# Where the first layer builds its rotary tables and its modulation columns: a new table of six and a moved call

## The chip, the cores and the metric

The kernel runs on one core of a Trainium2 chip. The metric is the device time of one execution in microseconds; the time before is the median of three runs. A profiled execution of the same kernel supplies the trace.

## What is computed

The reference is a trunk of two layers over 512 tokens of 1024 channels, all in f32. A layer, cut to what matters here:

```python
mod = c_act @ w_ada[l] + b_ada[l]
shift, scale, gate = jnp.split(mod, 3, axis=-1)
h = rms_norm(x, norm_g) * (1 + scale[:, None]) + shift[:, None]
a_qkv, a_z, m_cq, m_ckv, m_kr, m_z, merge = jnp.split(h @ w_in, SPLIT_IDX, axis=-1)
y_a = dilated_mixer(a_qkv, rel_bias) * jax.nn.silu(a_z)                # branch A
y_m = mla_mixer(m_cq, m_ckv, m_kr, ..., cos, sin) * jax.nn.silu(m_z)   # branch B
merged = g_a * (y_a @ w_out_a) + g_m * (y_m @ w_out_b)
x = x + gate[:, None] * (merged @ w_o)
```

`cos` and `sin` (the rotary tables) are read by branch B alone. `gate` is read at the layer's end, and the next layer's `scale` and `shift` when the next layer's `h` is made. None of the three is needed by branch A, which has 3 groups of 8 heads and is worked off in four pairs of heads.

## The kernel before, in words

**Stages.** Every f32 product is three TensorE products of high and low parts. A projection (`proj`, L166 is its matmul helper) takes 24 matmuls of 512 columns into a bank `pj`, of which there are two; its weights come by DMA into one of two tiles `stage`, and are split into `wh` and `wl` (three tiles each) by ScalarE, VectorE or GpSimd. Branch A of a layer runs: query and key of pair 0 (`a_qk(0)`), values (`a_v(0)`, whose later matmuls go to banks `pj` and `s`), a SiLU gate (`zgate`), attention of pair 0 (`a_attn(0)`), `a_qk(1)`, `a_attn(1)`, `a_qk(2)`, a gate, then branch B's latents (`m_latents`, the first reader of the rotary tables, L976 and L977), a second half of values, and pairs 2 and 3. Attention of a head ends in the one bank named `o`, which is copied out at L923 before it serves again.

**Modulation columns.** `ada_group` (L262) makes 512 modulation columns. In the first layer there are six such groups inside branch A: two of the layer's own gate (called gate 1 and gate 2 below) and four of the next layer's shift and scale (norm 1 to norm 4). A group loads eight tiles of 256 KB named `lat` (L272) and adds them up, scaled, into a ninth `lat` tile: the first two by ScalarE (L277) and VectorE, the rest by VectorE alone (L286, one instruction for each load). The sum is split into two more `lat` tiles by ScalarE (L203) and VectorE (L206). These are eleven requests to a pool of eight `lat` tiles. The group's `close` sums over the partitions with two matmuls into bank `o` (one pair, on TensorE's rows written `o<-lat,one_r`), copies a row out by ScalarE (L300), writes it to memory (`row`, L302), reads it back turned (`ada`, L304), and adds it up in small VectorE instructions (L306, L428, L444). Until its close has run, a group keeps three `lat` tiles: the sum and its two halves. Branch B's latents use the same pool.

`ada(i)` is called at eight places (i from 0 to 7). It first closes the group that is open, then opens `AP[l][i]` new ones; where it opens two, the first is closed as the second is opened. With `AP[0] = (1, 1, 2, 1, 2, 2, 0, 0)` the places open: gate 1; gate 2; norm 1 and norm 2; norm 3 (behind attention of pair 0); norm 4; none. The last close stands at `ada(5)`, behind attention of pair 1.

**Rotary tables.** `build_rope` (L555) loads the positions (L558) into a tile `pth`, and computes angles modulo a turn in some 26 VectorE instructions of 128x512 (L561 to L584), with `Abs` and two `Sin` on ScalarE (L581, L585, L586). It is called once, in the first layer, ahead of `a_attn(0)`.

**What sets the order.** The framework's scheduler places instructions by their place in the code and its own estimate of time; the built program is then fixed, and every engine, and SP's queue for all DMAs, works its instructions off in that order, waiting where one is not ready. A pool's tile, or a bank, goes to its users in the order of the code.

Of the kernel before, what the change touches and what calls it, by code (L numbers as in the profile page):

```python
# [41 lines left out]
SE = ('VV','VG','GVVV','AGGA')  # L42
SM = ('V','AA','V')
LOW = 300
AP = ((1, 1, 2, 1, 2, 2, 0, 0), (1, 0, 1, 1, 0, 1, 0, 2))
FULL = 3
NP = 2
NP2 = 1
# [42 lines left out]
def _split12(v, n):  # L91
    out = []
    for _ in range(n - 1):
        m, e = math.frexp(v)
        p = math.ldexp(math.floor(m * 4096.0), e - 12)
        out.append(p)
        v -= p
    out.append(float(np.float32(v)))
    return out
# [38 lines left out]
def trunk(ctx, tc, x, positions, w_ada, w_in, w_uq, w_ukv, w_out_a, w_out_b, w_o, rel_bias, vecs, cst, ohb, bmask, out):  # L138
# [17 lines left out]
    def t2(tag, dt=F32, shape=(128, 512)):  # L156
        return sb.tile(list(shape), dt, tag=tag, name=nm(tag), bufs=BUFS[tag])
# [50 lines left out]
    def hi_copy(dst, src, use):  # L208
        i = turn[use] = turn.get(use, -1) + 1
        if ENG[use][i % len(ENG[use])] == "A":  # L210
            A.activation(dst, src, AF.Copy)  # L211
        else:
            V.tensor_copy(dst, src)
# [300 lines left out]
    def later():  # L514
        return tc.issue_after(ada_end.ins)
# [9 lines left out]
    def build_bias():  # L525
# [17 lines left out]
        for pq in range(4):  # L543
            src = bass.AP(tensor=bv.tensor, offset=bv.offset + 127 - pq, ap=[[BW, 8], [-4, 32], [1, 256]])
            dma(btile[:, 32 * pq:32 * pq + 32, 0:256], src)
        for g in (1, 2):
            src = bass.AP(tensor=bv.tensor, offset=bv.offset + 8 * g * BW + UW + 256 * (g - 1) + 127,
                          ap=[[BW, 8], [-1, 128], [1, 128]])
# [6 lines left out]
    def build_rope(after):  # L555
        pi_ = t2("pth", I32)
        with later():
            dma(pi_, positions[0:1, :].to_broadcast([128, S]))  # L558
        pos = t2("ptl")
        with tc.issue_after(after.ins):  # L560
            V.tensor_copy(pos, pi_)  # L561
        fr = cs[:, 512:513]
        r = t2("pth")
        V.tensor_scalar(r, pos, fr, None, ALU.mult)
        e = t2("ptl")
        k = t2("ph")
        u = t2("pl")
        big = _split12(2.0 * math.pi * 2048.0, 4)
        two = _split12(2.0 * math.pi, 4)
        G.memset(e, 0.0)  # L570
        for period, parts in ((2.0 * math.pi * 2048.0, big), (2.0 * math.pi, two)):
            V.tensor_scalar(k, r, 1.0 / period, None, ALU.mult)
            V.tensor_scalar(k, k, MAGIC, None, ALU.add)
            V.tensor_scalar(k, k, -MAGIC, None, ALU.add)
            for i, pt in enumerate(parts):
                V.tensor_scalar(u, k, -pt, None, ALU.mult)
                dst = r if i < 2 else e
                V.tensor_tensor(dst, dst, u, ALU.add)
        V.tensor_tensor(r, r, e, ALU.add)
        ab = t2("ph")  # L580
        A.activation(ab, r, AF.Abs)  # L581
        V.tensor_scalar(ab, ab, -1.0, math.pi / 2, ALU.mult, ALU.add)
        lim = 3.1415925
        V.tensor_scalar(r, r, lim, -lim, ALU.min, ALU.max)  # L584
        A.activation(cos, ab, AF.Sin)  # L585
        A.activation(sin, r, AF.Sin)  # L586
# [15 lines left out]
    def layer(l, xT, hT):  # L602
# [29 lines left out]
        last_evac = [None]  # L632
# [74 lines left out]
        def v_evac(pj, n):  # L707
            v = t2("v", F32R)
            src = pj[:, :64 * n].rearrange("p (i e c) -> p i e c", e=2, c=64)
            b = v[:, :128 * n]  # L710
            hi = bass.AP(tensor=b.tensor, offset=b.offset, ap=[list(b.ap[0]), [256, n // 2], [192, 2], [1, 64]])
            lo0 = b[:, 64:128 * n]
            lo = bass.AP(tensor=b.tensor, offset=lo0.offset, ap=[list(b.ap[0]), [256, n // 2], [64, 2], [1, 64]])
            hi_copy(hi, src, "pv")
# [210 lines left out]
        def a_attn(j, qk, vt, z):  # L925
            stat = (small([128, 2, 4], "m0"), small([128, 2, 4], "l0"),
                    small([128, 2, 2, 4], "m12"), small([128, 2, 2, 4], "l12"))
            y = t2("yy")
            pps = a_scores(j, qk, stat)
            f0, f12 = a_factors(stat)  # L930
            for e in range(2):
                o = a_pv(e, pps[e], f0[:, e], f12[:, :, e], vt, 2 * (j % 2) + e)
                o_evac(y, e, o, True)
            (V if YZ[0] == "V" else G).tensor_tensor(y, y, z, ALU.mult)
            dma(yd[j], y)
# [198 lines left out]
        def ada(i):  # L1134
            if pend:
                pend.pop()()
            for _ in range(AP[l][i]):
                f = next(steps, None)
                if f is not None:
                    if pend:  # L1140
                        pend.pop()()
                    with tc.issue_after(h_last[0].ins):
                        pend.append(f())
# [3 lines left out]
        def gates(n):  # L1147
            for _ in range(n):
                ct = next(gq_, None)
                if ct is not None:  # L1150
                    merge_gate(ct)
# [7 lines left out]
        ada(1)  # L1159
        z = zgate(COL_AZ)  # L1160
        ada(2)
        if l == 0:
            build_rope(last_evac[0])
        a_attn(0, qk, vt, z[0])
        ada(3)
        qk = a_qk(1)
# [2 lines left out]
        ada(5)  # L1169
        gates(GP[0])  # L1170
        qk = a_qk(2)
        ada(6)
        gates(GP[1])
        z = zgate(COL_AZ + 256)
# [133 lines left out]
    class Final:  # L1308


        def __init__(self):
            v = vecs[R_F:R_Q, :]
            self.g = [t2("hTh") for _ in range(2)]
            for i in range(2):
                src = bass.AP(tensor=v.tensor, offset=v.offset + 512 * i, ap=[[0, 128], [1, 512]])
                dma(self.g[i], src)
# [33 lines left out]
    for l in range(DEPTH):  # L1350
        xT, hT = layer(l, xT, hT)
# [22 lines left out]
```

## Time and profile before

| | us |
| --- | --- |
| median of 3 runs (1441.36 to 1443.59) | 1442.48 |
| the profiled execution, its own time | 1442.84 |
| its span | 1441.0 |
| TensorE matmuls busy | 1343.7 (93%) |
| VectorE busy | 929.8 (65%) |
| ScalarE busy | 704.8 (49%) |
| GpSimd busy | 588.2 (41%) |

Times in the trace count from the span's start. An engine's row in the order of time gives start, duration, line, operation, output and inputs, and in brackets how long the engine stood idle before it and what ended the wait. The part of branch A that the change touches lies between 75 us (the values) and 281 us (the end of branch B's first projections).

### The profile page before, as it was taken

To read this page: it belongs to the slowest core of one execution; us is meant where nothing else is said; L and a number is where in the kernel's file an instruction comes from. 1 tells how busy PE (TensorE), PEld (TensorE's weight loads), DVE (VectorE), ACT (ScalarE), POOL (GpSimd) and SP (SyncE) were. 2 spreads that over 40 slices of the span, in tenths; PEclk is the share of its full clock that TensorE was granted. 3 is DMA by queue.
4 is the path that set the end of the run, shared out by engine and by line. 5 is a ranking of instruction groups with operands and counts; after the bars stand their busy time and mean duration, and the time that the engine had idled before them with its cause. 6 is when DMAs were issued, how large, how long until landed. Compare 5 with 4: busy or idle time off the path is not lost.

```text
span 1441.0 us, 21364 instructions
## 1 busy us (share of the span) xinstructions
PE 1343.7 (93%) x7327; PEld 1157.1 (80%) x7327; DVE 929.8 (65%) x2125; ACT 704.8 (49%) x1909; POOL 588.2 (41%) x431
## 2 busy tenths in 40 slices
PE   4988999999898999999989999999989898999997
PEld 3787877898787778888888988789878777888877
DVE  8788667435755777755699337744675586765553
ACT  3424664336556778621034266433654687862102
POOL 5423436334453333345444345543444333335430
PEclk7999999999999999999999999999999999999999
DMA  9776424323234323455754332323324332346541
GB/s 330 220 230 201 147 65 133 92 77 93 74 103 124 92 81 107 140 183 157 215 154 138 89 91 72 99 88 88 81 73 119 108 92 81 109 140 191 170 129 59
DMA packets 236677, 181.48 MB, mean 126 GB/s; under 512 B 16410, under 2 KB 204224, under 8 KB 236568
## 3 DMA queue, kind: packets, MB, share of 16 engines
q1 hardware_dynamic: 236568, 180.11, 42.4%
q8 instruction: 58, 0.95, 0.3%
q14 instruction: 51, 0.42, 0.1%
HBM read 150.60 MB, written 23.17 MB: 121 GB/s over the span
## 4 chain that ended last, share of the span: by engine, by line
PE 71%; DVE 13%; DMA 5%; issue 4%; ACT 3%; POOL 2%; SPq 1%; DVEq 0%; POOLq 0%; ACTq 0%
PE pj L166 50%; PE s L166 12%; PE o L166 5%; PE t L869 4%; DMA stage<-in_w_o 2%; DMA stage<-in_w_in 1%; DVE lat L286 1%; POOL wl L206 1%; DVE zs L286 1%; DMA ql<-pl 1%; DVE kb L667 1%; DVE p L392 1%; DMA lat<-in_w_ada 1%; DVE p L1101 1%; DVE yy L923 1%
## 5 line engine op out<-in xcount | busy, mean ns | idle before, releaser
L206 POOL TENSOR_TENSOR wl<-stage,wh 128x1024 fp32r<-128x1024 f32 (+1 forms) x134 | 316.9, 2366 | 381.6 <-ACT wh L203 194.9
L166 PE MATMUL pj<-hTh,wh 128*128 128x512 f32 (+1 forms) x864 | 344.6, 399 | 39.4 <-ACT gt L628 9.2
L166 PE MATMUL pj<-hTl,wh 128*128 128x512 f32 (+1 forms) x864 | 340.2, 395 | 0.0
L166 PE MATMUL pj<-hTh,wl 128*128 128x512 f32 (+1 forms) x848 | 335.3, 395 | 0.0
L166 PEld LDWEIGHTS pj<-hTh,wh 128*128 128x128 f32 x864 | 166.5, 193 | 75.1 <-issue 19.0
L166 PEld LDWEIGHTS pj<-hTl,wh 128*128 128x128 f32 x864 | 165.9, 192 | 32.0
L166 PEld LDWEIGHTS pj<-hTh,wl 128*128 128x128 f32 x848 | 163.5, 193 | 29.9 <-issue 0.3
L203 ACT ACTIVATE wh<-stage 128x1024 fp32r<-128x1024 f32 (+1 forms) x84 | 85.1, 1014 | 145.7 <-PE s L166 65.2
L872 DVE TENSOR_TENSOR ptl<-t,pth 128x512 fp32r<-128x512 f32 (+2 forms) x160 | 96.1, 618 | 41.7 <-ACT pth L211 41.0
L211 ACT ACTIVATE pth<-t 128x512 fp32r<-128x512 f32 (+2 forms) x160 | 81.7, 537 | 64.5 <-PE t L869 63.2
L166 PE MATMUL s<-kb,qh 128*128 128x256 f32 (+3 forms) x384 | 85.5, 316 | 8.7 <-DMA qh<-ph 5.8
L166 PE MATMUL o<-pth,v 128*64 128x128 f32 (+3 forms) x496 | 89.1, 257 | 2.1 <-DVE yy L923 1.1
L166 PEld LDWEIGHTS s<-kb,qh 128*128 128x128 f32 x384 | 65.7, 188 | 21.5 <-ACT qh L211 4.7
L1101 DVE CUSTOM_DVE_ANT_0 p<-s,cs 128x512 f32<-128x512 f32 (+3 forms) x128 | 58.6, 484 | 34.1 <-PE s L166 33.6
L869 PE MATMUL t<-eye_r,p 128*128 128x128 f32 x560 | 80.4, 274 | 0.1
L166 PE MATMUL o<-ptl,v 128*64 128x128 f32 (+2 forms) x320 | 76.4, 273 | 3.2 <-DVE ptl L872 3.1
L205 DVE CAST wh<-stage 128x1024 fp32r<-128x1024 f32 (+1 forms) x77 | 57.8, 751 | 32.4 <-PE pj L166 9.6
L166 PEld LDWEIGHTS o<-pth,v 128*64 128x64 f32 (+1 forms) x496 | 63.7, 151 | 7.7 <-DVE kh L923 1.6
L869 PEld LDWEIGHTS t<-eye_r,p 128*128 128x128 f32 x560 | 63.9, 140 | 5.4 <-DVE ptl L872 0.5
L166 PE MATMUL pj<-wh,hTh 128*128 128x256 f32 (+1 forms) x192 | 63.5, 332 | 1.8 <-DVE kb L667 1.8
L166 PE MATMUL pj<-wl,hTh 128*128 128x256 f32 (+1 forms) x192 | 62.7, 328 | 0.1
L166 PE MATMUL pj<-wh,hTl 128*128 128x256 f32 (+1 forms) x192 | 62.4, 325 | 0.0
(710 smaller groups left out, 3061.1 us busy)
## 6 DMA issues: line engine op xcount, KB each, us to landing
stage<-in_w_in SPq DMA_DIRECT2D x118, 512.0 KB
lat<-in_w_ada SPq DMA_DIRECT2D x64, 256.0 KB
v<-in_w_ada SPq DMA_DIRECT2D x32, 256.0 KB
stage<-in_w_in SPq DMA_DIRECT2D x32, 256.0 KB
gd<-gt SPq DMA_DIRECT2D x32, 256.0 KB
stage<-in_w_out_b SPq DMA_DIRECT2D x16, 512.0 KB
stage<-in_w_o SPq DMA_DIRECT2D x16, 512.0 KB
p<-yd SPq DMA_DIRECT2D x24, 256.0 KB
```

Source lines behind the costliest of these rows:

```text
L166: T.matmul(o, l, r, start=start, stop=stop, skip_group_check=True)
L203: A.activation(dst_h, src, AF.Copy)
L205: hi.tensor_copy(dst_h, src)
L206: (lo or G).tensor_tensor(dst_l, src, f32(dst_h), ALU.subtract)
L211: A.activation(dst, src, AF.Copy)
L286: V.scalar_tensor_tensor(acc, st, cact[:, k:k + 1], side if k == ne + np_ else acc, ALU.mult, ALU.add)
L392: (eng or V).tensor_tensor(sq[:, sl], xt[:, sl], xt[:, sl], ALU.mult)
L667: last_evac[0] = V.tensor_tensor(lo[r, :, e], src[r], f32(h[r, :, e]), ALU.subtract)
L869: T.transpose(tp[:, 128 * b:128 * b + 128], s, eye)
L872: V.tensor_tensor(lo[:, :n], tp[:, :n], f32(h[:, :n]), ALU.subtract)
L923: V.tensor_tensor(yo, oa, yo, ALU.add)
L1101: V.tensor_tensor_reduce(pt, o, mask[:, 512 - n:512], 1.0, -3e38, ALU.add, ALU.max, m[:, qb:qb + 1])
```

## The change

Two things in the first layer. The table that says how many modulation groups each `ada(i)` opens becomes `(1, 0, 1, 0, 1, 1, 1, 1)`: gate 1 at `ada(0)`, gate 2 at `ada(2)`, norm 1 to norm 4 at `ada(4)` to `ada(7)`, each closed at the next call (norm 4 just ahead of `m_latents`). And `build_rope` is called behind `a_qk(2)`, with the last copy of that projection as the point from which it may start.

```diff
-AP = ((1, 1, 2, 1, 2, 2, 0, 0), (1, 0, 1, 1, 0, 1, 0, 2))
+AP = ((1, 0, 1, 0, 1, 1, 1, 1), (1, 0, 1, 1, 0, 1, 0, 2))
@@ in layer()
         ada(1)
         z = zgate(COL_AZ)
         ada(2)
-        if l == 0:
-            build_rope(last_evac[0])
         a_attn(0, qk, vt, z[0])
         ada(3)
         qk = a_qk(1)
@@
         ada(5)
         gates(GP[0])
         qk = a_qk(2)
+        if l == 0:
+            build_rope(last_evac[0])
         ada(6)
         gates(GP[1])
         z = zgate(COL_AZ + 256)
```

What that does to the built program is shown at two places. First place, the values `a_v(0)`, on TensorE, right behind the close of gate 1 (bank `o_1008`); `s_858` and `s_859` are banks of the later values with weights `wh_863`, `s_1126` is a score of pair 0, and `pj_772` is a block of the earlier values. This is a piece of the difference:

```order
 L166 MATMUL o_1008<-lat_728,one_r 2x512
 L166 MATMUL o_1008<-lat_729,one_r 2x512
+L166 MATMUL s_858<-wh_863,hTh_210 128x512
+L166 MATMUL s_858<-wh_863,hTl_211 128x512
+L166 MATMUL s_859<-wh_863,hTh_210 128x512
+L166 MATMUL s_859<-wh_863,hTl_211 128x512
+L166 MATMUL s_1126<-kh_516,qh_485 128x256
+L166 MATMUL s_1126<-k2z_441,qh_485 128x256
 L166 MATMUL pj_772<-wh_734,hTh_210 128x256
 L166 MATMUL pj_772<-wh_734,hTl_211 128x256
```

The first matmuls on `wh_863` have moved ahead of the blocks `pj_772` and `pj_800`, that is ahead of 48 matmuls of 256 columns that stood between.

The same stage on ScalarE, at the copies of the later values (`v_984`, `v_987`), again a piece of the difference:

```order
 L203 ACTIVATE wh_956<-stage_953 128x1024
-L581 ACTIVATE ph_1229<-pth_1200 128x512
 L211 ACTIVATE v_984<-pj_856 128x2x2x64
-L585 ACT_TABLE_LOAD
-L585 ACTIVATE cos<-ph_1229 128x512
-L586 ACTIVATE sin<-pth_1200 128x512
+L203 ACTIVATE lat_1718<-lat_1693 128x512
 L211 ACTIVATE v_987<-pj_856 128x2x2x64
```

The rotary tables' three functions and their table load have left the gap between the two copies; the split of norm 1's sum stands there now.

Second place, on TensorE, the close of norm 2 of before (`o_1585`; `pj_2359` is a key projection of pair 2 and `pj_2394` the block behind it, in which the close of norm 3, `o_1841`, stands in the same way), a piece of before:

```order
L166 MATMUL pj_2359<-hTl_223,wh_2355 128x512
L166 MATMUL pj_2359<-hTh_224,wh_2355 128x512
L166 MATMUL o_1585<-lat_1192,one_r 2x512
L166 MATMUL o_1585<-lat_1193,one_r 2x512
L166 MATMUL pj_2359<-hTh_224,wl_2356 128x512
```

and the closes of norm 1 to norm 4 of after on TensorE, behind attention of pair 1 (`pj_2603` and `pj_2639` are the first and second half of branch B's query latent):

```order
L166 MATMUL pj_2603<-hTl_225,wh_2599 128x512
L166 MATMUL o_2072<-lat_1718,one_r 2x512
L166 MATMUL o_2072<-lat_1719,one_r 2x512
L166 MATMUL o_2367<-lat_2108,one_r 2x512
L166 MATMUL o_2367<-lat_2109,one_r 2x512
L166 MATMUL o_2475<-lat_2403,one_r 2x512
L166 MATMUL o_2475<-lat_2404,one_r 2x512
L166 MATMUL o_2549<-lat_2511,one_r 2x512
L166 MATMUL o_2549<-lat_2512,one_r 2x512
L166 MATMUL pj_2639<-hTh_210,wh_2635 128x512
```

Where a close stood among projection matmuls before, four closes follow each other now with nothing between.

The closes on SP's queue, with what each instruction waits for (`PE` for TensorE, `DVE` for VectorE, `Activation` for ScalarE, `Pool` for GpSimd, `DMAHW` for an earlier transfer). In before, the loads of norm 4 (`lat_1859` to `lat_1874`, its third to eighth) behind the closes of norm 2 (`row_1589`) and norm 3 (`row_1845`):

```order
L272 DMA lat_1859<-in_w_ada 128x2x256 [waits PE_49]
L272 DMA lat_1862<-in_w_ada 128x2x256 [waits DVE_49]
L302 DMA row_1589<-lat_1167 1x512 [waits Activation_49]
L272 DMA lat_1865<-in_w_ada 128x2x256 [waits DMAHW6_49]
L304 DMA ada_1591<-row_1589 128x4x1 [waits DMAHW7_49,DMAHW5_49]
L272 DMA lat_1868<-in_w_ada 128x2x256 [waits DMAHW0_49]
L272 DMA lat_1871<-in_w_ada 128x2x256 [waits DMAHW3_49,DMAHW1_49,DVE_49]
L272 DMA lat_1874<-in_w_ada 128x2x256 [waits DMAHW4_49,DMAHW2_49,DVE_49]
L302 DMA row_1845<-lat_1596 1x512 [waits Activation_49]
```

In after, the loads of norm 3 (`lat_2385` to `lat_2400`, its third to eighth) behind the closes of norm 1 (`row_2076`) and norm 2 (`row_2371`):

```order
L272 DMA lat_2385<-in_w_ada 128x2x256 [waits DMAHW1_49,PE_49]
L302 DMA row_2076<-lat_1693 1x512 [waits DMAHW2_49,Activation_49]
L935 DMA yd<-yy_1726 128x512 [waits Pool_49]
L272 DMA lat_2388<-in_w_ada 128x2x256 [waits DVE_49]
L304 DMA ada_2078<-row_2076 128x4x1 [waits DMAHW5_49,DMAHW2_49]
L302 DMA row_2371<-lat_2083 1x512 [waits DMAHW6_49,Activation_49]
L272 DMA lat_2391<-in_w_ada 128x2x256 [waits DMAHW7_49]
L272 DMA lat_2394<-in_w_ada 128x2x256 [waits DMAHW0_49,PE_49]
L304 DMA ada_2373<-row_2371 128x4x1 [waits DMAHW6_49,DMAHW1_49]
L272 DMA lat_2397<-in_w_ada 128x2x256 [waits PE_49]
L272 DMA lat_2400<-in_w_ada 128x2x256 [waits DMAHW3_49]
```

The group whose loads stand between two closes was norm 4 and is norm 3 now: six of its eight loads are in and behind the closes of norm 1 and norm 2; the loads of norm 4 stand in the same way behind the close of norm 3 (`row_2479`, `ada_2481`).

## Rows read from the trace of the kernel before

**Rows 1.** Busy time by stretch: PE, PEld, DVE, ACT, POOL, clock, DMA share, GB/s

```profile
121.30:131.00 9.70, 3.90 (x10) 3.14 (x11) 8.88 (x17) 6.10 (x14) 4.73 (x2) 0.65 0.46 139
...
264.00:281.00 17.00, 17.00 (x95) 13.98 (x94) 5.61 (x8) 5.99 (x9) 6.73 (x8) 1.00 0.28 78
```

**Rows 2.** TensorE in order of time: start, us, instruction [idle before it, what ended that]

```profile
82.95 0.62 PE L166 MATMUL o<-lat,one_r 128*2 128x512 f32 x2
...
90.09 0.63 PE L166 MATMUL s<-wh,hTh 128*128 128x512 f32 x1 [0.21 <-ACT wh L203]
...
92.52 0.62 PE L166 MATMUL s<-wl,hTh 128*128 128x512 f32 x1 [1.57 <-POOL wl L206]
...
127.10 0.76 PE L166 MATMUL pj<-hTh,wh 128*128 128x512 f32 x1 [5.82 <-DVE v L715]
...
154.63 0.51 PE L166 MATMUL s<-kb,qh 128*128 128x256 f32 x2 [0.46 <-DVE x L800]
...
188.42 0.60 PE L166 MATMUL pj<-hTh,wh 128*128 128x512 f32 x1 [2.10 <-DVE kb L667]
...
228.37 0.47 PE L166 MATMUL pj<-hTh,wh 128*128 128x512 f32 x1 [2.37 <-DVE kb L667]
```

**Rows 3.** The chain that ended last: matmuls after two stalls, and undisturbed ones

```profile
127.10 7.37 PE pj L166 x24
...
397.92 10.02 PE pj L166 x31
...
651.71 5.44 PE pj L166 x24
```

**Rows 4.** ScalarE in order of time, at the end of the values

```profile
124.66 0.63 ACT L585 ACTIVATE cos<-ph 128x512 f32<-128x512 f32 x1 [3.88 <-DVE ph L582]
125.20 0.61 ACT L586 ACTIVATE sin<-pth 128x512 f32<-128x512 f32 x1
125.99 0.66 ACT L211 ACTIVATE v<-pj 128x256 fp32r<-128x256 f32 x2 [0.18 <-DVE v L715]
```

**Rows 5.** The chain that ended last, where the later values' weights arrive

```profile
80.73 2.82 SPq L740
83.60 5.27 DMA stage<-in_w_in
88.98 1.07 ACT wh L203
```

**Rows 6.** VectorE by line, 80 to 127 us: busy, mean ns | idle before

```profile
L576 DVE TENSOR_SCALAR pl<-ph 128x512 f32<-128x512 f32 x8 | 4.1, 512 | 0.1
...
L578 DVE TENSOR_TENSOR pth<-pth,pl 128x512 f32<-128x512 f32 x4 | 2.7, 687 | 0.1
```

**Rows 7.** The chain that ended last, one close and the load behind it

```profile
142.03 0.57 ACT lat L300
...
142.61 1.78 DMA row<-lat
...
144.42 0.57 SPq L304
...
145.05 3.65 DMA lat<-in_w_ada
```

**Rows 8.** The `lat` tiles from 215 to 285 us: ns min/median/max, first and last start

```profile
L286 DVE SCALAR_TENSOR_TENSOR lat<-lat,cact,lat x7: 736/747/1616, 220.1 to 235.3; 128x512 f32<-128x512 f32 x7
...
L166 PE MATMUL o<-lat,one_r x6: 397/397/398, 219.0 to 275.5; 128*2 128x512 f32 x6
...
L203 ACT ACTIVATE lat<-lat x1: 632/632/632, 236.8 to 236.8; 128x512 fp32r<-128x512 f32 x1
L206 DVE TENSOR_TENSOR lat<-lat,lat x1: 675/675/675, 238.9 to 238.9; 128x512 fp32r<-128x512 f32 x1
```

**Rows 9.** ScalarE, then VectorE: bank `o` copied out after pair 1's attention

```profile
269.48 1.08 ACT L211 ACTIVATE yy<-o 64x512 f32<-64x512 f32 x1 [6.13 <-PE o L166]
...
270.59 1.06 DVE L923 TENSOR_TENSOR yy<-o,yy 64x512 f32<-64x512 f32 x1 [5.21 <-ACT yy L211]
```

## The prediction

> **What bounds the kernel now.** I read the busy shares first: TensorE's matmuls take 93% of the span, so a microsecond counts only where TensorE stands still or runs at its lower clock. Next came TensorE in order of time through the changed part. It stands idle for 5.82 us before 127.10, for 2.10 and 2.37 us ahead of two query and key blocks, and for half a microsecond or less in small waits; behind the close of gate 1 (two matmuls of 0.62 us, done by 83.57) the later values' first matmul starts only at 90.09, but it waited 0.21 us, since 48 other matmuls stand in between [rows 2]. In the stretch around 127 the granted clock is 0.65, and 24 matmuls behind the stall last 7.37 us where 24 undisturbed ones last 5.44 [rows 1, 3]: of TensorE's two levels, 1.2 and 2.4 GHz, part of the block ran at the lower one. The place where the new order puts four closes, behind attention of pair 1, has no idle time at all: TensorE is busy 17.00 of 17.00 us at full clock, VectorE 5.61 and the DMA engines at a share of 0.28 [rows 1]. Whatever the change makes TensorE wait for there is lost whole.
>
> **The removed work: rotary tables off the values.** The wait before 127.10 is ended by VectorE's correction of a value block, which waits for ScalarE's copy of it; ScalarE stood waiting 3.88 us for the angle, then made cosine and sine (0.63 and 0.61), then the copy [rows 2, 4]. VectorE's steps of 512 to 687 ns stand in the same stretch [rows 6]. With the functions gone from between the copies the copy no longer waits. I count the whole stall, 5.82, and the slow clock behind it, 7.37 − 5.44 = 1.93: −7.75. What is late next there is the copy of the block itself, 0.66 for two copies; TensorE can be fed about 2 us before it would stop again, so I keep half the stall (−3.9) as the lower bound of the gain. Two waits of 0.46 in pair 0's scores, behind VectorE (the first stands in [rows 2]), go with it: −0.9. The waits of 2.10 and 2.37 are VectorE's work on key blocks, untouched by the change; 0.
>
> **A new wait at the later values.** The matmuls on `wh_863` now stand right behind the close of gate 1. Their weights are issued at 80.73 (2.82), land at 88.87 and are split by 90.05 [rows 5]. Nothing in the change makes them earlier: the queue ahead of them is the same. TensorE therefore stops from 83.57 to 90.09, 6.5 us, where it now works on the blocks that stood between. Of the waits there today 0.21 and 1.57 go, since their cover is ahead of them now [rows 2]: 6.5 − 1.8 = +4.7. The clock falls after a stall of this length as after the one at 127, 1.93 on either account, and there is a short slow stretch today behind the 1.57, so nothing further is added. The bounds are 0 (the loads are issued earlier, as fewer `lat` loads are queued) and +6.6. Front in sum: −7.75 − 0.9 + 4.7 = −3.9, between −9 and +2.
>
> **The moved work: four closes in a row.** After, each group holds three `lat` tiles until its close, of eight. Norm 1 and norm 2 can be summed early, but they then hold six. Norm 3 finds two tiles: its third load waits for TensorE's close of norm 1, its sixth and seventh for that of norm 2, and SP's queue has the row and the turned row of both closes between them, each waiting for ScalarE or for a transfer; everything behind, the weight loads of the next blocks too, stands in that queue. Norm 4 stands in the same way to norm 3. Closes may not go ahead of attention of pair 1 either, since bank `o` is handed out in code order. In before, such a round lay beside projections, which filled TensorE; after, the close of the next group is TensorE's next instruction, and it waits for the round to end. The round's price, step by step. From close of norm 1 to close of norm 3: pair 0.62 [rows 2], ScalarE's copy 0.57, row 1.78, issue of the turned row 0.57 [rows 7]; the second row's issue 0.4 and its row and turned row again 2.35; then two more load issues, 0.8 (SP works off one in some 0.4); landing 3.65 [rows 7]; VectorE's last addition 0.75, the split 0.63 and 0.68 [rows 8]. With 0.4 for the first row's issue this is 13.2. From close of norm 3 to close of norm 4 there is one row and turned row, and four load issues (1.6): 0.62 + 0.57 + 0.4 + 2.35 + 1.6 + 3.65 + 0.75 + 1.31 = 11.25. With the last pair, 0.62, the sum is 25.1. The four pairs' own time, some 0.5 each, was paid before in other places: −2.0, so 23.1.
>
> Two more terms. Ahead of the first of these closes bank `o` must be copied out: ScalarE 1.08 and VectorE 1.06 [rows 9], today beside TensorE's other work, of which three matmuls (0.7) are left in front. That is 1.5 alone, 3.2 with rotary steps in front on VectorE; I take 2.5. And after a stall the lower clock: 1.93 for 24 matmuls as at 127, or 3.0 (31 matmuls in 10.02 against 31 times 5.44/24, which is 7.03) [rows 3]; I take 2.4. The wall: 23.1 + 2.5 + 2.4 = +28.0.
>
> Bounds. From below: a landing of 2 instead of 3.65 twice, and no second wait for a row, take off 3.3 and 2.3, and the loads may have been queued well enough for another 2: about 20. From above: in before a round lasted from 219.0, the close of norm 2, to 239.6, the split of the group behind it [rows 8], 20.6 us, with ScalarE and VectorE queues in its way. The rotary steps (26 of about 0.5, 687 ns at most [rows 6]) now stand on VectorE among the additions. Two such rounds would be +41. I take the sum of the steps, since VectorE is busy only 5.61 of 17 us there [rows 1] and, when TensorE stands still, it has nothing else to do; a rotary step between two additions fits into the 0.4 to 0.6 us in which the loads follow each other.
>
> On landing, the trace has 3.65 us for 256 KB [rows 7]. The Trainium skill, "DMA: Bandwidth & Descriptors", section "Anatomy of one DMA — SWDGE (gpsimd) path", gives about 2.0 us plus the bytes at 436 GB/s, an estimate of 2.6 us for this size; the time would then be about 2 us below mine, near 1465. The measured number decides.
>
> **Sum.** −3.9 + 28.0 = +24.1 on the profiled execution's 1442.84 (span 1441.0, median of the runs 1442.48, so no correction is needed): 1467. About 0.2% of this kernel, 2.9 us, is what a measurement can tell from no change.
>
> **Rivals.** Long rounds: each of the two is paced by the rotary steps and by ScalarE, as the 20.6 us round of before was [rows 8]. For it speaks that this is the one round the trace has whole; against it that its engines were working for attention then. It decides if an addition waits for more than one rotary step: +33 to +41, 1476 to 1483. Short rounds: landings and rows shorter on idle DMA engines (share 0.28 today [rows 1]), and the front's waits all gone with no new one: −8 + 20, 1453 to 1458.
>
> Faster: the spread does what the words say. Closes of norm 1 to norm 3 are fed early enough that each finds its sum ready, TensorE never waits for a round, and the values' stall of 7.75 is a gain that outweighs the 4.7 at 83.57: 1442.8 − 3.9 = 1439. It decides if the loads of a group can be issued before the earlier group is closed; against it stand the three tiles that a pending group keeps and the waits for TensorE in SP's queue. The trace so far has its rounds hidden only because projections stand between closes. Beside it stands the Trainium skill, same page, section "Rules for kernel authors": issue a transfer early, compute, and wait for it late, so that its fixed cost overlaps. By that rule a later close is the better one; the pool takes the early issue away here, and no row of before shows it given back.
>
> No change: the front's gain of up to 9 meets a wall of under 12, which would need a single round in place of two; the order of the closes speaks against it.
>
> **How the numbers follow.** Forecast (1460 to 1475) 0.62; long rounds 0.16; short rounds 0.15; faster 0.04; no change 0.02; 0.01 for beyond. The predicted time is the forecast's 1467. The range, 8 in 10, takes in most of both neighbouring cases: 1454 to 1480. Slower by over 0.2%: 0.94; within: 0.02; faster: 0.04.
>
> **What would show it.** In the profile of the changed kernel TensorE waits twice for some 10 to 13 us, each time ahead of a pair of matmuls on a `lat` sum and ended by VectorE's or ScalarE's split, between 265 and 300 us, with the row and load issues filling SP's queue in these gaps and a slice with the lower clock behind them. At 83.6 a wait of about 6.5 us is ended by ScalarE's split of `wh`. The stall at 127 is gone, and cosine and sine stand behind pair 1's attention. Wrong would be the forecast if the four pairs stand on TensorE without idle time between them; the step that fails is then the tiles' hold. If the wait at 83.6 is missing, the front's sum is 4.7 lower; if the gaps are 20 us each, the pace of the additions was mis-sized.

## The result, and the profile of the changed kernel

| | before | changed |
| --- | --- | --- |
| median, us | 1443.03 (1441.36 to 1445.07) | 1467.61 (1464.35 to 1469.44) |
| profiled execution, its own time | 1442.84 | 1466.26 |
| its span | 1441.0 | 1464.5 |

The ratio is 1.0171 (95% interval 1.0153 to 1.0189): slower by 24.6 us, where 24.1 were forecast. First the part of branch A in two stretches of time, before and changed (us, busy time and instructions of TensorE's matmuls and weight loads, VectorE, ScalarE, GpSimd; granted clock, DMA share, GB/s). Of before:

```profile
60.00:260.00 200.00, 183.58 (x932) 155.23 (x931) 149.02 (x326) 98.31 (x276) 78.94 (x51) 0.96 0.50 148
260.00:300.00 40.00, 40.00 (x252) 35.70 (x251) 17.53 (x30) 13.12 (x20) 14.88 (x13) 1.00 0.30 83
```

Changed:

```profile
60.00:260.00 200.00, 187.34 (x972) 160.83 (x971) 121.27 (x282) 91.46 (x267) 79.11 (x56) 0.97 0.45 132
260.00:300.00 40.00, 14.34 (x68) 9.15 (x67) 29.59 (x56) 11.58 (x18) 5.56 (x3) 0.66 0.42 123
```

Up to 260 us TensorE stands still for 200 − 187.34 = 12.7 us instead of 16.4: 3.7 won. In the next 40 us it stands still for 25.7, where before it never did. These are TensorE's waits, changed kernel, in order of time (start, us, instruction, in brackets the idle time before it and what ended that); they answer to [rows 2]:

```profile
72.98 0.47 PE L166 MATMUL pj<-hTh,wh 128*128 128x512 f32 x1 [0.53 <-DVE ql L685]
...
87.82 0.82 PE L166 MATMUL s<-wh,hTh 128*128 128x512 f32 x1 [5.42 <-ACT wh L203]
...
123.86 0.47 PE L166 MATMUL pj<-hTh,wh 128*128 128x512 f32 x1 [1.18 <-DVE v L715]
...
215.31 0.47 PE L166 MATMUL pj<-hTh,wh 128*128 128x512 f32 x1 [2.76 <-DVE kb L667]
...
264.34 0.63 PE L166 MATMUL o<-lat,one_r 128*2 128x512 f32 x2 [1.68 <-DVE yy L923]
265.63 0.62 PE L166 MATMUL o<-lat,one_r 128*2 128x512 f32 x2 [0.67 <-ACT lat L300]
278.47 0.59 PE L166 MATMUL o<-lat,one_r 128*2 128x512 f32 x1 [12.21 <-ACT lat L203]
279.47 0.59 PE L166 MATMUL o<-lat,one_r 128*2 128x512 f32 x1 [0.42 <-DVE lat L206]
290.47 1.31 PE L166 MATMUL o<-lat,one_r 128*2 128x512 f32 x2 [10.41 <-ACT lat L203]
```

The stall at the values has shrunk from 5.82 to 1.18, and one of 5.42 has come behind gate 1's close. The four closes wait for a copy of bank `o` (1.68), a row's copy (0.67) and two rounds (12.21 and 10.41). A round is what TensorE waits for between two closes: the rows of the earlier close, the loads of the next group behind them, that group's last additions and its split. What filled the first round, on SP's queue and then on VectorE (GpSimd's row stands last):

```profile
265.00 0.37 SPq L272 DMA_DIRECT2D lat<-in_w_ada  x1
265.61 0.25 SPq L302 DMA_DIRECT2D row<-lat  x1
...
267.33 0.36 SPq L304 DMA_DIRECT2D ada<-row  x1
267.80 0.31 SPq L302 DMA_DIRECT2D row<-lat  x1
...
269.70 0.37 SPq L304 DMA_DIRECT2D ada<-row  x1
270.12 1.01 SPq L272 DMA_DIRECT2D lat<-in_w_ada  x2
```

```profile
264.92 1.76 DVE L286 SCALAR_TENSOR_TENSOR lat<-lat,cact,lat 128x512 f32<-128x512 f32 x1
266.61 2.56 DVE L576 TENSOR_SCALAR pl<-ph 128x512 f32<-128x512 f32 x1
...
277.01 0.74 DVE L286 SCALAR_TENSOR_TENSOR lat<-lat,cact,lat 128x512 f32<-128x512 f32 x1
...
266.10 2.78 POOL L206 TENSOR_TENSOR wl<-stage,wh 128x1024 fp32r<-128x1024 f32 x1
```

SP has issued norm 3's last load by 271.13, behind the rows of two closes. VectorE's last addition starts only at 277.01: between 260 and 280 VectorE is busy for 19.6 of the 20 us, with rotary steps among the additions. The second round by the chain that ended last (start, us, what):

```profile
280.10 0.58 ACT lat L300
280.70 0.25 SPq L302
...
281.97 0.46 SPq L304
...
283.08 4.25 DMA lat<-in_w_ada
...
287.42 0.76 DVE lat L286
288.21 0.76 DVE lat L286
289.00 0.76 DVE lat L286
289.79 0.64 ACT lat L203
```

That is the predicted chain: a row, its turned row, the loads behind it, the last additions and the split.

For the comparisons below I worked out, for each profile, TensorE's idle time, and what the lower clock took: in stretches of 10 us the busy time, times the share of the clock that was not granted, summed (an estimate, since the granted clock is a mean). All figures are in us.

| kernel | idle, 60 to 260 us | lost to the clock there | idle, 260 to 300 us | lost to the clock there |
| --- | --- | --- | --- | --- |
| before | 16.4 | 6.2 | 0.0 | 0.0 |
| changed | 12.7 | 4.9 | 25.7 | 3.1 |
| changed, second profile | 14.8 | 3.5 | 25.6 | 4.5 |
| table of six alone | 16.6 | 0.9 | 21.2 | 3.2 |
| table of six alone, second profile | 16.7 | 1.5 | 22.5 | 4.0 |
| tables' move alone | 14.5 | 3.5 | 4.8 | 1.5 |
| changed, twelve tiles | 15.9 | 6.0 | 5.2 | 2.3 |
| twelve tiles, tables back | 16.3 | 3.6 | 0.7 | 0.0 |
| three closes in a row | 15.7 | 4.6 | 12.9 | 3.6 |
| twelve tiles, tables in the middle | 22.5 | 7.4 | 4.1 | 1.4 |

From before to changed the four columns sum to −3.7 − 1.3 + 25.7 + 3.1 = +23.8; the profiled executions differ by 23.4.

### The profile page after: what moved, and what is told of

The parts are those of the page before. It is cut to its first block, busy times and chain, and to the rows that moved or that the text cites. A ratio compares the mean times of both kernels' runs of the same rounds, so it can differ in the third digit from the quotient of the medians.

```text
span 1464.5 us, 21373 instructions
## 1 busy us (share of the span) xinstructions
PE 1344.1 (92%) x7327; PEld 1157.2 (79%) x7327; DVE 925.9 (63%) x2125; ACT 705.0 (48%) x1909; POOL 586.4 (40%) x431
## 4 chain that ended last, share of the span: by engine, by line
PE 70%; DVE 13%; DMA 5%; ACT 4%; issue 4%; SPq 2%; POOL 1%; DVEq 0%; POOLq 0%; ACTq 0%
PE pj L166 49%; PE s L166 12%; PE o L166 5%; PE t L869 3%; DMA stage<-in_w_o 2%; DVE lat L286 1%; ACT p L806 1%; POOL wl L206 1%; DMA lat<-in_w_ada 1%; DVE ptl L872 1%; ACT p L1103 1%; DVE kb L667 1%; DMA ql<-pl 1%; DVE wh L205 1%; DVE p L1101 1%
```

## The experiments

Theory: the loss is the row of four closes, whose rounds come from the tiles that a pending group holds; the rotary tables' move is a small gain in front. Rivals: the tables' steps on VectorE make the rounds, or the place behind the attention does, whatever tiles there are.

**The table of six alone** (`build_rope` where it was before).

```diff
-AP = ((1, 1, 2, 1, 2, 2, 0, 0), (1, 0, 1, 1, 0, 1, 0, 2))
+AP = ((1, 0, 1, 0, 1, 1, 1, 1), (1, 0, 1, 1, 0, 1, 0, 2))
```

> Only the table of six is changed; the rotary tables stay ahead of pair 0's attention. Theory (the four closes in a row are the whole loss, the moved tables the whole gain in front): four closes still stand together behind pair 1's attention, two rounds of 10 to 13 us each; the stall of about 6 us at the values stays, and no stall of 5.4 us behind gate 1's close comes. With the rotary steps gone from the first round VectorE no longer paces its additions, so that round is some 2 to 3 us shorter than the 12.2 of the changed kernel. Time 1466 to 1472. Rival (the rotary steps on VectorE make the rounds long): the rounds fall under 8 us each and the time is at most 1460.

Measured: 1459.97 us (ratio 1.0128, 1.0103 to 1.0154), below the theory's range, and by its figure on the rival's side. Both rounds are there, however: 9.35 and 10.33 us of idle time. The stall of 5.6 us at the values is there too, and none of 5.4 behind gate 1's close. As forecast, the first round is 2.9 us shorter than with the rotary steps; its additions now wait for their loads, where in the changed kernel VectorE itself was late. So the rounds are not the tables'; the missed 6 us led to the next two runs.

**The same two kernels again, side by side.**

> The changed kernel once more, beside the kernel with only the table of six changed. Theory (moving the tables wins 3.7 us of waits in front and loses 4.5 us in the rows of closes, so it is worth nothing): 1464 to 1470, and at most 3 us above the other. Rival (the 7.6 us between the two that the first runs showed are the tables'): again 6 to 9 us above the other.

> The kernel with only the table of six changed once more. Theory (its 1460.0 held some 3 us of luck with TensorE's clock in front: 0.9 us were lost there to the lower clock, 4.1 in the kernel that differs only in who issues the rows): 1462 to 1466. Rival: 1458 to 1462 as before.

Measured: changed 1467.03 (1.016, 1.0133 to 1.0188), table alone 1465.51 (1.0149, 1.0119 to 1.0179). The theory's figures hold: the two differ by 1.5 us, within their scatter (1463.94 to 1469.59 and 1461.93 to 1468.13), and the first 1460.0 was 5.5 us lower than the same kernel's second median. It was not luck with the clock in front, as I had guessed: its two profiles lose 0.9 and 1.5 us there. The spans of these two profiles differ by 8.6 us though the program is the same from end to end: 2.1 arise at the closes and 3.5 between 800 and 1130 us, in idle time and clock together; the rest is spread. The rounds of the second profile, on TensorE, and two of the additions in the first round, on VectorE:

```profile
265.25 0.62 PE L166 MATMUL o<-lat,one_r 128*2 128x512 f32 x2
266.98 0.62 PE L166 MATMUL o<-lat,one_r 128*2 128x512 f32 x2 [1.10 <-ACT lat L300]
277.13 1.31 PE L166 MATMUL o<-lat,one_r 128*2 128x512 f32 x2 [9.53 <-ACT lat L203]
289.88 1.31 PE L166 MATMUL o<-lat,one_r 128*2 128x512 f32 x2 [11.43 <-ACT lat L203]
...
274.45 0.75 DVE L286 SCALAR_TENSOR_TENSOR lat<-lat,cact,lat 128x512 f32<-128x512 f32 x1 [0.31 <-DMA lat<-in_w_ada]
275.62 0.75 DVE L286 SCALAR_TENSOR_TENSOR lat<-lat,cact,lat 128x512 f32<-128x512 f32 x1 [0.42 <-DMA lat<-in_w_ada]
```

**The rotary tables' move alone** (the table of six as before).

```diff
-        if l == 0:
-            build_rope(last_evac[0])
         a_attn(0, qk, vt, z[0])
@@
         qk = a_qk(2)
+        if l == 0:
+            build_rope(last_evac[0])
```

> Only the call of the rotary tables is moved; the table of six is that of before, and closes stand among projections. Theory: the stall of 5.8 us before 127 goes with the slow stretch behind it, a stall of some 5.4 us comes behind gate 1's close (the matmuls on wh_863 stand there in this kernel too), and the tables cost nothing at their new place: 3 to 6 us faster, 1437 to 1440. Rival (branch B waits for the late tables, or VectorE's additions do): 1443 or more.

Measured: 1443.39 us (1.0008, 0.9995 to 1.002): no gain, the rival's figure. TensorE's waits in it:

```profile
87.81 0.82 PE L166 MATMUL s<-wh,hTh 128*128 128x512 f32 x1 [5.45 <-ACT wh L203]
...
124.15 0.47 PE L166 MATMUL pj<-hTh,wh 128*128 128x512 f32 x1 [1.65 <-DVE v L715]
...
148.96 0.51 PE L166 MATMUL s<-kb,qh 128*128 128x256 f32 x2 [2.51 <-DVE x L800]
...
271.29 0.47 PE L166 MATMUL pj<-hTh,wh 128*128 128x512 f32 x1 [0.99 <-DVE lat L960]
277.03 0.38 PE L166 MATMUL pj<-wh,hTh 128*128 128x256 f32 x1 [1.83 <-DVE lat L960]
280.95 0.39 PE L166 MATMUL pj<-wl,hTh 128*128 128x256 f32 x1 [1.99 <-DVE wl L206]
```

The stall at the values has shrunk to 1.65, much as in the changed kernel, and the 5.45 behind gate 1's close, which the table alone does not bring, belongs to this edit. At its new place the work holds VectorE up where branch B's latents need it (0.99, 1.83 and 1.99), and in pair 0's scores the wait has grown (2.51). Idle time in the two stretches is 19.3 us together, where before had 16.4, and the clock takes 5.0 instead of 6.2. So the waits eat the gain.

**Twelve `lat` tiles in the changed kernel.**

```diff
-kb=4, v=12, lat=8, p=8, ph=2, pl=2,
+kb=4, v=12, lat=12, p=8, ph=2, pl=2,
```

> The changed kernel with twelve lat tiles in place of eight; nothing else. In its program all loads of norm 3 and norm 4 stand ahead of the first of the four closes, of which the first two are next to each other and the others 24 and 22 projection matmuls apart. Theory (a pending group's three tiles hold back the loads): no round of 10 us is left, at most 4 us of waits at the four closes; with the front's gain of 7 to 8 us the time is 1434 to 1441. Rival (the place behind the attention and bank o is the cause, however many tiles there are): waits of over 15 us stay there, 1455 or more.

Measured: 1444.73 us (1.0024, 1.0011 to 1.0037). The rounds are gone: idle time behind pair 1's attention falls from 25.7 to 5.2 us and the time by 22.9 us, with nothing changed in the code but the number of tiles. The built program also moves, as the expectation says: 24 and 22 matmuls stand between the later closes. It is not they that hide the rounds, since no close has one to wait for: the last of the six groups is summed and split on VectorE at 242.56, 30 us ahead of the first of the four closes. The range was missed by 3.7 us on the slow side, and what is left is no round. TensorE, then VectorE:

```profile
272.37 1.01 PE L166 MATMUL o<-lat,one_r 128*2 128x512 f32 x2 [4.35 <-DVE yy L923]
274.05 1.01 PE L166 MATMUL o<-lat,one_r 128*2 128x512 f32 x2 [0.67 <-ACT lat L300]
...
241.88 0.68 DVE L206 TENSOR_TENSOR lat<-lat,lat 128x512 fp32r<-128x512 f32 x1
...
267.89 2.60 DVE L576 TENSOR_SCALAR pl<-ph 128x512 f32<-128x512 f32 x1
270.53 0.69 DVE L578 TENSOR_TENSOR pth<-pth,pl 128x512 f32<-128x512 f32 x1
271.25 1.06 DVE L923 TENSOR_TENSOR yy<-o,yy 64x512 f32<-64x512 f32 x1
```

Bank `o`'s copy stands behind rotary steps on VectorE.

**A control: twelve tiles in the kernel before.**

> The kernel before with twelve lat tiles, a control for the two kernels that have them. Theory (the tiles held nothing back in before, its closes stand among projections): within 3 us of before, 1439.5 to 1445.5. Rival (four more tiles move loads and cost or save time by themselves): outside of that.

Measured: 1441.80 us (0.9997, 0.997 to 1.0024). Four more tiles do nothing by themselves that can be told, within 0.3%.

**Twelve tiles, the new table, the rotary tables back** (both edits from above, without the move).

> The new table of six, twelve lat tiles, the rotary tables built where they were before. Theory (the tiles alone make the rounds, the tables alone make the stalls of 5.6, 4.1 and 4.4 us that the kernel with twelve tiles still has): none of these three, no round of over 4 us, 1431 to 1438. Rival (twelve tiles cost time elsewhere, or the late closes cost it): 1440 or more.

Measured: 1439.53 us (0.9986, 0.9969 to 1.0003), 1.5 above the theory's range. The three stalls named and the rounds are gone, but the stall at the values is back with the tables (4.35 us). It is 5.2 us below the same kernel with the tables moved.

**The tables in the middle.** The changed kernel with twelve tiles, the call behind pair 0's attention:

```diff
         a_attn(0, qk, vt, z[0])
+        if l == 0:
+            build_rope(last_evac[0])
         ada(3)
         qk = a_qk(1)
@@
         qk = a_qk(2)
-        if l == 0:
-            build_rope(last_evac[0])
         ada(6)
```

> The changed kernel with twelve lat tiles and the rotary tables built behind pair 0's attention instead of behind pair 2's projections. Theory (the 4.35 us for bank o's copy and the 1.1 us behind it in the kernel with twelve tiles are rotary steps queued ahead on VectorE): those two fall under 1.5 us together, the 5.5 us behind gate 1's close stay; time 1438 to 1442, 3 to 5 us under the 1444.7 of that kernel. Rival (the copy waits for something else): 3 us or more of wait stay there, 1443 or more.

Measured: 1452.20 us (1.0054, 1.0035 to 1.0072). The forecast of the time fell. TensorE still waits for the copy of bank `o`, though less: 2.24, and none of the 0.67 behind it. No rotary step stands ahead of the copy now; the 2.24 are about its own two halves, 1.06 by ScalarE and then 1.06 by VectorE. The rotary steps have gone to pair 1's stage, and idle time between 60 and 260 us rises from 15.9, with twelve tiles and the late tables, to 22.5. The waits there, of 2.43, 1.73, 2.84 and 2.94, are ended by VectorE's splits of keys and queries, among which the rotary steps stand, or by ScalarE. No place tried for the tables was free.

**Three closes in a row** (against the table of six alone, the tables where they were before).

```diff
-AP = ((1, 0, 1, 0, 1, 1, 1, 1), (1, 0, 1, 1, 0, 1, 0, 2))
+AP = ((1, 0, 1, 1, 1, 1, 1, 0), (1, 0, 1, 1, 0, 1, 0, 2))
```

> The table (1, 0, 1, 1, 1, 1, 1, 0), the rotary tables where they were before, eight lat tiles: norm 1 is closed among pair 2's projections, and three closes instead of four stand in a row behind pair 1's attention. Theory (each group whose loads must wait for an earlier close is a round of its own; norm 3 can now be summed with the five tiles that norm 2 leaves it, norm 4 can't): one round of 9.5 to 12 us instead of two, 9 to 12 us less idle time between 260 and 300 us than the 21.2 of the kernel with only the table changed; time 1448 to 1455. Rival (the row of closes costs as a whole, two rounds stay): 1457 or more.

Measured: 1456.07 us (1.0088, 1.006 to 1.0117), 1 us above the range, which rested on the first 1460.0; against the second median of the table alone, taken beside it, it is 9.4 us less. One round, as forecast:

```profile
269.99 0.62 PE L166 MATMUL o<-lat,one_r 128*2 128x512 f32 x2 [1.31 <-DVE yy L923]
271.28 0.99 PE L166 MATMUL o<-lat,one_r 128*2 128x512 f32 x2 [0.67 <-ACT lat L300]
282.89 1.31 PE L166 MATMUL o<-lat,one_r 128*2 128x512 f32 x2 [10.62 <-ACT lat L203]
```

Norm 2 and norm 3 are closed next to each other without a round between, norm 4 waits for one. In this table and in the table of six alone a round is the price of each group that must wait for an earlier close.

**The closes apart, with the tables moved and not moved.** The same edit of the table for both, with eight tiles; in the second the call of `build_rope` stays where it was before.

```diff
-AP = ((1, 0, 1, 0, 1, 1, 1, 1), (1, 0, 1, 1, 0, 1, 0, 2))
+AP = ((1, 0, 1, 1, 2, 1, 0, 0), (1, 0, 1, 1, 0, 1, 0, 2))
```

> The changed kernel with the table (1, 0, 1, 1, 2, 1, 0, 0): eight lat tiles as before, but gate 2 and norm 1 and 2 are closed behind pair 0's attention with projections between, norm 3 and norm 4 in branch B's projections, 16 matmuls apart. Theory (rounds cost nothing while projections fill TensorE): at most 5 us of waits at the closes, time 1435 to 1444. Rival (three tiles held by a group make any table of eight tiles lose a round of 10 to 13 us): 1447 or more.

> The table (1, 0, 1, 1, 2, 1, 0, 0) of the kernel with the closes apart, but the rotary tables built where they were before, ahead of pair 0's attention. Theory (moving the tables brings the stall of 5.4 us behind gate 1's close and some 3 us of waits for VectorE at pair 1's attention and the latents, and saves nothing that the table of six alone doesn't save): no stall over 2 us at 83 us, none of 5.8 us at the values, though the tables are back; 5 to 8 us faster than that kernel's 1439.5, 1431 to 1436. Rival (the stall at the values comes back with the tables): 1438 to 1444.

Measured: 1439.47 us (0.9985, 0.997 to 0.9999) with the tables moved, 1439.76 (0.9986, 0.9963 to 1.0009) with the tables back. The first theory held in its time, not in its bound of 5 us: at the closes TensorE waits 3.67 (for a row's copy, which stands behind other work on ScalarE) and 2.54 (for the copy of bank `o`), 6.2 together. Eight tiles lose no round where projections stand between closes. The second fell by its figure: the move costs nothing and brings nothing here, because the stall at the values comes back with the tables (5.70 us) as the rival had it, and takes the place of the waits that go. Both are some 3 us below before, about what can be told from no change; the first one's interval just excludes it. They are the fastest kernels here, with the one with twelve tiles and the tables back. TensorE's waits at the closes with the tables moved, then the one at the values with the tables back:

```profile
216.48 1.01 PE L166 MATMUL o<-lat,one_r 128*2 128x512 f32 x2 [3.67 <-ACT lat L300]
...
270.46 0.62 PE L166 MATMUL o<-lat,one_r 128*2 128x512 f32 x2 [2.54 <-DVE yy L923]
```

```profile
125.29 0.77 PE L166 MATMUL pj<-hTh,wh 128*128 128x512 f32 x1 [5.70 <-DVE v L715]
```

**Rows issued by ScalarE.** The table alone, with row and turned row of the four norm closes on ScalarE's queue instead of SP's (`ncl` counts the closes; the third to the sixth are norm 1 to norm 4):

```diff
-                dma(row, acc[:1, :])
+                ncl[0] += 1
+                q = A.dma_start if 3 <= ncl[0] <= 6 else dma
+                q(row, acc[:1, :])
                 res = small([128, 4], "ada")
-                dma(res, row[0].rearrange("(i p) -> p i", p=128))
+                q(res, row[0].rearrange("(i p) -> p i", p=128))
```

> The kernel with only the table of six changed, but row and turned row of the four norm closes are issued by ScalarE, so that SP's queue holds loads alone there. Theory (SP waits for the rows of two closes with the loads of the next group behind it, as in the prediction's steps): the first round falls from 9.35 us of idle to 6.5 to 7.5, the second from 10.33 to 9 to 9.8, the time from 1460.0 to 1455 to 1458. Rival (the loads wait for the tiles and land in their own time whatever stands between): both rounds stay within 0.7 us, 1459 to 1461.

Measured: 1465.83 us (1.0175, 1.0136 to 1.0215), the same as the second median of the table alone; rounds of 9.39 and 10.75 us. So taking the rows from SP's queue gains nothing. It does not show that the rows cost nothing, since VectorE's queue waits for them, and longer than before (VectorE, the same kernel; its line numbers are a few higher):

```profile
286.64 0.16 DVE L309 TENSOR_TENSOR Bc<-ada,vec 128x2 f32<-128x2 f32 x1 [3.18 <-DMA ada<-row]
...
287.57 3.11 DVE L287 SCALAR_TENSOR_TENSOR lat<-lat,cact,lat 128x512 f32<-128x512 f32 x4
```

Five additions of the next group stand behind the turned row's addition, which waited 3.18 us; with the rows on SP's queue it waited 0.83 and 1.89 in the two profiles of the table alone. So part of the wait has changed its queue. What a round would be with the rows on neither queue was not tried.

## Why the prediction was right

**Front.** Forecast −3.9; idle time fell by 3.7 and the clock's share by 1.3 (by 1.6 and 2.7 in the second profile). The single terms: the stall at the values fell by 4.64 of the 5.82 counted, between the stated bounds, and the matmuls behind it run undisturbed (48 in 11.17 us, where 24 undisturbed ones take 5.44). The new stall behind gate 1's close measured 5.42 where 6.5 was forecast, and the removed 0.21 and 1.57 are gone. Behind it the lower clock takes 2.3 between 80 and 100 us, by the estimate above, where it took 1.4 in before behind the 1.57: not quite nothing further, as the prediction had it. The rest was not foreseen: the wait of 1.73 at 74 us fell to 0.53, and of the waits of 2.10, 1.06 and 2.37 two are left, of 2.76 and 2.58. The prediction's reading had left out the 1.73 and the 1.06, where it speaks of half a microsecond or less. The gain belongs to the tables' move: with the table of six alone the front's idle time is as before (16.6 and 16.7 us), with the move alone it is 14.5, with both 12.7 and 14.8.

**The wall.** Forecast +28.0; 25.7 of idle time and 3.1 of clock, 28.8 in all (30.1 in the second profile). The cause is shown by the tiles: with twelve instead of eight all sums are ready ahead of the closes and 20.5 of the 25.7 us are gone, with a control that twelve do nothing in before. The steps: copy of bank `o` 1.68 for 2.5; close 1 to close 3, 264.34 to 278.47, 14.1 for 13.2; close 3 to close 4, 12.0 for 11.25, with a landing of 4.25 instead of 3.65; the clock 3.1 for 2.4.

**What was mis-sized.** The first round's sum came out for a partly wrong reason. SP's part took 6.8 us (264.34 to 271.13) where its steps make 7.5, but then the rotary steps, which the forecast let fit between the additions, held the last ones up: that is the rival with long rounds, at part of its price. Without them the round's idle time is 9.35 or 9.53 instead of 12.21. One rotary step alone, the one of 2.56 at 266.61, is 2.1 us longer than its like. And the late tables cost more elsewhere than the nothing that was counted for them: some 4.8 us at the latents where no closes stand (the move alone).

That the sum met the median within 0.6 us is luck: the single terms were off by about 1 us, both ways, and two medians of one kernel lay 5.5 us apart.

**The rivals.** Faster and no change failed on the tiles, as argued. Short rounds failed too: the landing measured 4.25 us, not less than 3.65 (the 2.6 estimated in the prediction comes from a figure for transfers that GpSimd issues, and these are SP's), and the front has a new wait of 5.42. A row of three closes, with one round, still loses 12.4 us against the runs of before beside it.

## What to carry to other kernels

A group that keeps buffers until a late step is paid when the next group's loads wait for those buffers: count what a pending group holds against the pool before closes are moved, since spreading the groups' starts over a stage doesn't spread their ends. If the pool can't grow, leave other work between the ends (with eight tiles and projections between the closes the time was at or a little below that of before). Work that is moved off one engine's stall goes into another place of the same in-order queue. Here no other place for the rotary steps paid: the time stayed the same (the move alone, the closes apart) or rose, with twelve tiles by 5 us at the late place and by some 12 in the middle.

## What was not expected of the hardware

VectorE's instructions lasted longer beside GpSimd's: a `TENSOR_SCALAR` of 128x512 that takes 0.43 took 2.56 us at 266.61, beside GpSimd's subtraction of 2.78 us, and an addition of 0.74 took 1.76. The twelve-tile kernel has the like (2.60 at 267.89). It is so in all fourteen profiles: of VectorE's f32 instructions of 128x512 (`TENSOR_SCALAR`, `TENSOR_TENSOR`, `SCALAR_TENSOR_TENSOR`) none of the 2174 that no GpSimd `TENSOR_TENSOR` overlaps lasts over 0.9 us, while 333 of the 1424 that one overlaps last over 1 us. The delay is not of the record alone, since the work behind it is late as well: in the twelve-tile kernel the next step and the copy of bank `o` follow the long step without a gap, and TensorE's pair follows the copy. No run here takes GpSimd's work away, so why it happens, and why only to some of them, stays open.

The loss to the lower clock isn't the same each time after nearly the same stall: with 5.5 to 5.8 us at the values it was, between 60 and 260 us, 0.9 and 1.5 in two profiles of one kernel, 4.1 in the kernel that differs only in who issues the rows, and 6.2 in before. The same kernel's median moved from 1459.97 to 1465.51 between two sets of runs. A difference of 5 us between two medians was not safe here before it was repeated.
